# Gate and up weights of a mixture of experts in rows of 8 KB and units of 1 MB, with doubled slots and a router in natural column order

## The chip, the cores and the metric

The kernel runs on one core of a Trainium2 chip; the chip's other cores are idle. A core has TensorE (PE; its weight loads are listed as PEld), VectorE (DVE), ScalarE (ACT), GpSimd (POOL) and SyncE (SP), and 16 DMA engines that move data between HBM and the on-chip memory SBUF. The metric is the device time of one execution in microseconds (us), as the median of several runs.

## What is computed

The reference is one layer of a decoder trunk in float32, on 256 tokens of width 2048: adaLN vectors from `c`, four kinds of attention (A to D) that share one input and one output projection, and a mixture of 16 experts of width 512, of which each token uses 2. Cut to what matters here:

```python
sh1, sc1, g1, sh2, sc2, g2 = jnp.split(c_act @ ada_w[l] + ada_b[l], 6, axis=-1)
...
h = rmsnorm(x, norm2_g[l]) * (1.0 + sc2[:, None]) + sh2[:, None]
x = x + g2[:, None] * moe_ffn(h, router_w, router_bias, exp_w_gate[l], exp_w_up[l], exp_w_down[l])
...
aff = jax.nn.sigmoid((t @ router_w).astype(jnp.float32))
...
for e in range(N_EXPERTS):
    he = jax.nn.silu(t @ w_gate[e]) * (t @ w_up[e])
    y = y + combine[:, e:e + 1] * (he @ w_down[e])
```

The weights are read once: each expert has a gate, an up and a down matrix of 4.194 MB each, 201 MB for the 16; the other weights are some 165 MB.

## The kernel before

**The stream of weights.** All large weights come over SP's DMA queue in units of 512 KB (a tile of 128 partitions x 1024 float32, `UNIT`). The list `units` (lines 268 to 315) has their order: adaLN weights `ada_w` with the early projection pieces, then projections (`uw`), compression weights and the other adaLN vectors (`usc`, `ush`, `ug`) mixed, then the output projection (`uo`) with the last adaLN vector, and at the end, pair of experts by pair, `pair_units`: gate and up (`ugu`), then down (`udh`). The class `Stream` (line 101) hands out slots: `pump` takes the next unit of the list and a free slot and issues the load; `done` gives the slot back once the unit's last reader has been written into the program, and the load into a slot waits on the chip until those readers have run. The framework lays out the order on each engine's queue from a timeline that it works out itself, so SP's order follows the list only roughly. SP executes its queue in order, and eight loads can be under way.

**Slots.** `ring1` has 11 slots of one unit (`RING`, line 352). When an attention branch's score bias `T` isn't needed any more, its space becomes one slot of two units, three times (line 987). After attention come three slots `s0` to `s2` (line 1130), then five that are used once, in `yhl`, `yo`, `ga` and `gb` (`ONCE`, line 1223), whose space gets its proper use during the first pair, and after the output projection `y0` to `y2` (line 1261). A slot of two units is given back when both halves are done.

**Gate and up.** Line 181 views a gate matrix as 8 blocks c of 256 rows; partition p holds rows 2p and 2p + 1 of the block, one run of 4 KB in HBM. So k = 2c + i is the product over rows 256c + 2p + i. `GUORDER` (line 57) is the order of blocks c and matrices g (0 gate, 1 up). For each block and each of the pair's two experts there is one unit; the two experts' products run in the two halves of PE's columns (line 1423).

**Permuted columns.** Since k stands for every second row, all that meets these weights has the same order of the 2048 columns: the scale and shift `A2`, `B2` of the second norm (adaLN vectors `sc2`, `sh2`, made by `ada_cols` with a permuted bias `abP`), the router weights (`wrP`, permuted by four products with the identity in `permuted`, lines 407 and 1137), and the transposes of the router, which read every second column of `xt` (lines 1176 and 1199). After the router, `xsplit` (line 1333) scales x and splits it into two parts `xh` and `xl`; `xview` reads every second column. `gather` (line 1372) collects, for four experts at once, the tokens of each by a product with a 0/1 matrix, in steps of two k, and applies `A2` and `B2`; in the first pair these steps are mixed into the gate and up products.

**The end of a pair.** Silu and product, transposes `hpT`, the down products `dn` in four blocks of 512 columns, and `scatter` (line 1453), which adds the result to `xt`. The last pair's last block goes in pieces of 128 columns. `fgr`, the last gain, is spread over the partitions during the last pair, into two free slots.

Of the kernel before, what the change touches and what calls it, by code (L numbers as in the profile page):

```python
# [23 lines left out]
NE = 16  # L24
# [22 lines left out]
ONCE = ("yhl", "yhl", "yo", "ga", "gb")  # L47
# [9 lines left out]
GUORDER = [(c, g) for c in range(6) for g in range(2)] + [(6, 0), (7, 0), (6, 1), (7, 1)]  # L57
# [43 lines left out]
class Stream:  # L101
# [5 lines left out]
    def add_slots(self, pool, names, n=1):  # L107

        self.free += [(pool, t, n) for t in names]
        self.pump()  # L110

    def room(self, name):
        if isinstance(self.free[0], list):
            t, slot = self.free.pop(0)
            return t, slot
        pool, tag, n = self.free.pop(0)
        t = pool.tile([128, max(n, 1) * UNIT], F32, name=name, tag=tag, bufs=2 if tag == "yhl" else 1)
        slot = [pool, tag, n, n]
        self.free[0:0] = [[t[:, UNIT * i:UNIT * i + UNIT], slot] for i in range(1, n)]
        return t[:, 0:UNIT], slot  # L120

    def pump(self):
        while self.free and self.pos < len(self.units):
            key, load = self.units[self.pos]
            self.pos += 1
            if key is None:
                load()
                continue
            t, slot = self.room("u" + "".join(c for c in str(key) if c.isalnum()))
            load(t)  # L130
            self.live[key] = (t, slot)
# [18 lines left out]
def hybrid_trunk_kernel(  # L150
# [30 lines left out]
    gateT = exp_w_gate[0].rearrange("e (c p i) f -> p c e (i f)", p=128, i=2)  # L181
    upT = exp_w_up[0].rearrange("e (c p i) f -> p c e (i f)", p=128, i=2)
# [40 lines left out]
    def pair_units(p):  # L223
# [14 lines left out]
        us = [((("gu", p), c, g, e), mkg(c, g, e)) for c, g in GUORDER for e in range(2)]  # L238
# [113 lines left out]
    stream.add_slots(ring1, [f"r{i}" for i in range(RING)])  # L352
# [50 lines left out]


    abP = const.tile([128, 3, 16], F32, name="abP")

    def permuted(dst, src, m, tag):
        pp = ps(tag, [128, 2, 8, m], name="perm")
        for h in range(2):
            for i in range(2):  # L410
# [987 lines left out]
    for p in range(NP):  # L1398
# [3 lines left out]
        for n, (c, g) in enumerate(GUORDER):  # L1402
            if p == 0 and c < 6 and g == 0 or p == 0 and c == 6:
                next(first, None)
            if (c, g) == (6, 0):
                weights(p)
# [236 lines left out]
```

## Time and profile before

| | us |
|---|---|
| median of 3 runs (1059.71 to 1063.89) | 1061.38 |
| the profiled execution | 1063.05 |
| its span | 1061.3 |
| PE busy in the span | 965.6 (91%) |
| DVE, ACT busy | 516.6, 330.6 |
| read from HBM | 367.91 MB, 349 GB/s over the span |
| chain that ended last, by engine | PE 57%, DMA 28%, DVE 8%, ACT 3% |

The profile is of one execution. Times in it are us from the start of its span. The line of GB/s has 40 equal slices of 26.5 us. "The chain" is the work that ended last, followed back step by step to what released it. A wait is put down to what ended it. SPq is SP's queue of DMA issues. "x8" is a count. A tile is named without its numbers: `ugu` are all gate and up units.

### The profile page before, as it was taken

What the parts mean: (1) busy time and instruction counts of PE and PEld (TensorE: products, weight loads), DVE (VectorE), ACT (ScalarE), POOL (GpSimd) and SP (SyncE); (2) the same over time, 40 slices, a digit from 0 to 9 for tenths busy, and PEclk for the clock granted to TensorE, in tenths of its full rate; (3) what the DMA queues carried; (4) which work ended last, traced back from release to release, by engine and by line L of the source; (5) the groups of instructions that cost most, each with busy time, mean ns of one, the idle gap of its engine ahead of it and who ended that gap; (6) DMA issues with size and microseconds to landing.
All of it is one profiled execution on the core that took longest, in us unless ns stands there. A gap on an engine that the chain in (4) does not pass through costs nothing.

```text
span 1061.3 us, 16623 instructions
## 1 busy us (share of the span) xinstructions
PE 965.6 (91%) x6433; PEld 587.5 (55%) x6433; DVE 516.6 (49%) x1093; ACT 330.6 (31%) x710; POOL 4.8 (0%) x14
## 2 busy tenths in 40 slices
PE   5999989899889999979998999999989896998884
PEld 1677778898778986646794434433343332432222
DVE  2444557996899999544345232414133130413115
ACT  3333334455565757634334100100020000200013
POOL 0000000000000000000000000000000000000000
PEclk9999999899989999989998999999999999999997
DMA  9999999996999999999743999999999999999994
GB/s 330 356 358 358 353 318 304 332 360 217 318 352 327 334 348 385 349 304 382 274 150 114 410 408 409 409 409 409 409 409 409 409 408 409 409 410 409 409 387 135
DMA packets 172031, 371.18 MB, mean 350 GB/s; under 512 B 13561, under 2 KB 92322, under 8 KB 171690
## 3 DMA queue, kind: packets, MB, share of 16 engines
q1 hardware_dynamic: 170944, 368.42, 94.6%
q10 hardware_dynamic: 938, 1.61, 0.4%
q8 instruction: 53, 0.87, 0.3%
q14 instruction: 32, 0.26, 0.1%
q0 software_dynamic: 64, 0.02, 0.0%
HBM read 367.91 MB, written 2.10 MB: 349 GB/s over the span
## 4 chain that ended last, share of the span: by engine, by line
PE 57%; DMA 28%; DVE 8%; ACT 3%; issue 3%; SPq 0%; DVEq 0%; ACTq 0%
DMA ugu<-in_exp_w_up_dram 10%; DMA ugu<-in_exp_w_gate_dram 7%; PE dn L170 7%; PE acc L537 5%; PE acc L538 4%; PE acc L539 4%; DMA udh<-in_exp_w_down_dram 4%; PE ada L170 3%; PE gatep L170 3%; PE upp L170 3%; PE oacc L541 3%; PE oacc L542 3%; PE oacc L543 3%; DMA uw<-in_w_in_dram 2%; PE pg L1381 2%
## 5 line engine op out<-in xcount | busy, mean ns | idle before, releaser
L537 PE MATMUL acc<-Hh,wlo 128*128 128x256 f32 x512 | 148.2, 300 | 6.6 <-DVE wlo L562 4.2
L538 PE MATMUL acc<-Hl,whi 128*128 128x256 f32 x512 | 147.4, 290 | 0.0
L539 PE MATMUL acc<-Hh,whi 128*128 128x256 f32 x512 | 146.6, 289 | 0.0
L173 PE MATMUL gatep<-ugu,xg 128*64 128x512 f32 x364 | 122.6, 600 | 0.0
L173 PE MATMUL upp<-ugu,xg 128*64 128x512 f32 x368 | 121.2, 595 | 0.0
L170 PE MATMUL dn<-udh,heT 128*64 128x512 f32 x242 | 112.1, 600 | 2.9 <-DVE heT L1451 2.6
L537 PEld LDWEIGHTS acc<-Hh,wlo 128*128 128x128 f32 x512 | 98.7, 198 | 18.9 <-DVE wlo L562 6.7
L173 PE MATMUL dn<-udh,heT 128*64 128x512 f32 x234 | 108.3, 600 | 0.0
L538 PEld LDWEIGHTS acc<-Hl,whi 128*128 128x128 f32 x512 | 100.2, 196 | 3.4 <-issue 2.9
L539 PEld LDWEIGHTS acc<-Hh,whi 128*128 128x128 f32 x512 | 99.7, 195 | 2.5 <-issue 2.2
L1434 DVE TENSOR_TENSOR he<-upp,sg 128x128 f32<-128x128 f32 x32 | 7.1, 284 | 170.6 <-PE upp L173 167.9
L562 DVE TENSOR_TENSOR wlo<-uw,whi 128x1024 fp32r<-128x1024 f32 x62 | 75.7, 1221 | 15.8 <-ACT whi L560 15.6
L170 PE MATMUL gatep<-ugu,xg 128*64 128x512 f32 x144 | 75.2, 611 | 7.6 <-DMA ugu<-in_exp_w_gate_dram 7.6
L170 PE MATMUL upp<-ugu,xg 128*64 128x512 f32 x144 | 73.6, 600 | 7.8 <-DMA ugu<-in_exp_w_up_dram 7.8
L560 ACT CAST whi<-uw 128x1024 fp32r<-128x1024 f32 x62 | 64.8, 1047 | 48.7 <-PE acc L539 21.4
L1464 DVE TENSOR_TENSOR xt<-xt,sco 128x512 f32<-128x512 f32 (+1 forms) x70 | 42.3, 639 | 54.7 <-PE sco L1463 54.2
L1513 ACT CAST yhl<-yo 128x512 fp32r<-128x512 f32 x31 | 19.2, 618 | 159.7 <-DVE yo L1507 153.3
L170 PEld LDWEIGHTS dn<-udh,heT 128*64 128x64 f32 x242 | 30.0, 136 | 62.1 <-issue 49.1
L562 DVE TENSOR_TENSOR wlo<-uo,whi 128x1024 fp32r<-128x1024 f32 x31 | 37.8, 1223 | 51.2 <-ACT whi L560 49.4
L541 PE MATMUL oacc<-wlo,Oh 128*128 128x512 f32 (+1 forms) x160 | 57.8, 362 | 0.0
L542 PE MATMUL oacc<-whi,Ol 128*128 128x512 f32 (+1 forms) x160 | 56.0, 350 | 0.0
L543 PE MATMUL oacc<-whi,Oh 128*128 128x512 f32 (+1 forms) x160 | 55.9, 350 | 0.0
(397 smaller groups left out, 1730.0 us busy)
## 6 DMA issues: line engine op xcount, KB each, us to landing
ugu<-in_exp_w_up_dram SPq DMA_DIRECT2D x128, 512.0 KB, 10.2
ugu<-in_exp_w_gate_dram SPq DMA_DIRECT2D x127, 512.0 KB, 10.2
udh<-in_exp_w_down_dram SPq DMA_DIRECT2D x119, 512.0 KB, 10.2
usc<-in_ada_w_dram SPq DMA_DIRECT2D x64, 512.0 KB, 7.8
ush<-in_ada_w_dram SPq DMA_DIRECT2D x62, 512.0 KB, 7.1
uw<-in_w_in_dram SPq DMA_DIRECT2D x62, 512.0 KB, 6.0
ug<-in_ada_w_dram SPq DMA_DIRECT2D x56, 512.0 KB, 7.2
uo<-in_w_out_dram SPq DMA_DIRECT2D x31, 512.0 KB, 9.6
```

The costliest lines, as they stand in the source:

```text
L170: ins = op(*args, **kw).ins
L173: ins = op(*args, **kw).ins
L537: ins = mm(o, wl, hh, start=first, stop=False)
L538: mm(o, wh, hl, start=False, stop=False)
L539: mm(o, wh, hh, start=False, stop=last)
L541: ins = mm(o, hh, wl, start=first, stop=False)
L542: mm(o, hl, wh, start=False, stop=False)
L543: mm(o, hh, wh, start=False, stop=last)
L560: A.copy(hi, w)
L562: V.tensor_tensor(lo, w, hi[:].bitcast(F32), OP.subtract)
L1381: mm(pg[:, i, :], x_[:, t, i, 128 * c:128 * c + 128], oh4[q][:, t].rearrange("p e s -> p (e s)"), start=n == 0, stop=n == 3)
L1464: V.tensor_tensor(y(t, cs), y(t, cs), o, OP.add)
```

## The change

It does five things.

- Gate and up matrices are viewed as 4 blocks of 512 rows, with four rows to a partition: one run of 8 KB in HBM. A unit is 1 MB and fills a slot of two units; down units stay at 512 KB. `GUORDER` becomes (0, gate), (0, up), (1, gate), (1, up), (2, gate), (3, gate), (2, up), (3, up).
- `Stream` knows sizes. `ring1` has 5 slots of two units and one of one unit; `s0`, `y0` and `y1` are slots of two units, and so are `yhl` and `g2r`, which are used once. The total of 23 units in slots that come back stays; those used once are 4 units, not 5. A unit of 512 KB takes half a slot of two units, or the single slot.
- Where nothing fits a gate or up unit, `pump` stops until something does.
- The router works in natural column order. The permutation of the router weights and of three vectors at the start is gone; instead `A2` and `B2` are permuted after the adaLN vectors are known, each by 16 products with 32 columns of the identity. The router's transposes read 128 adjacent columns.
- `xview` reads every fourth column, `xh` and `xl` are laid out in four quarters, and a step of `gather` still makes two k; in the first pair the steps now stand before k = 0, 2 and so on of the gate blocks.

Its core:

```diff
-ONCE = ("yhl", "yhl", "yo", "ga", "gb")
+ONCE = ("yhl", "g2r")
...
-GUORDER = [(c, g) for c in range(6) for g in range(2)] + [(6, 0), (7, 0), (6, 1), (7, 1)]
+GUORDER = [(c, g) for c in range(2) for g in range(2)] + [(2, 0), (3, 0), (2, 1), (3, 1)]
...
+    def room(self, name, size=1):
+
+        for at, slot in enumerate(self.free):
+            if isinstance(slot, list) if size == 1 else not isinstance(slot, list) and slot[2] == size:
+                break
+            if size == 1 and not isinstance(slot, list):
+                break
+        else:
+            return None
+        if isinstance(slot, list):
+            return self.free.pop(at)
+        pool, tag, n, once = self.free.pop(at)
+        t = pool.tile([128, n * UNIT], F32, name=name, tag=tag, bufs=1)
+        slot = [pool, tag, n, once, n // size]
+        if size == n:
+            return [t[:], slot]
+        self.free[at:at] = [[t[:, UNIT * i:UNIT * i + UNIT], slot] for i in range(1, n)]
+        return [t[:, 0:UNIT], slot]
...
-        slot[3] -= 1
-        if not slot[3] and slot[2]:
-            self.free.append(tuple(slot[:3]))
+        slot[4] -= 1
+        if not slot[4] and not slot[3]:
+            self.free.append(tuple(slot[:4]))
             self.pump()
...
-    gateT = exp_w_gate[0].rearrange("e (c p i) f -> p c e (i f)", p=128, i=2)
-    upT = exp_w_up[0].rearrange("e (c p i) f -> p c e (i f)", p=128, i=2)
+    gateT = exp_w_gate[0].rearrange("e (c p i) f -> p c e (i f)", p=128, i=4)
+    upT = exp_w_up[0].rearrange("e (c p i) f -> p c e (i f)", p=128, i=4)
...
-        us = [((("gu", p), c, g, e), mkg(c, g, e)) for c, g in GUORDER for e in range(2)]
+        us = [((("gu", p), c, g, e), mkg(c, g, e), 2) for c, g in GUORDER for e in range(2)]
...
-    stream.add_slots(ring1, [f"r{i}" for i in range(RING)])
+    stream.add_slots(ring1, [f"r{i}" for i in range(RING // 2)], 2)
+    stream.add_slots(ring1, [f"r{i}" for i in range(RING // 2, RING // 2 + RING % 2)])
...
-    permuted(abP[:, 0, :].unsqueeze(2), abT[:, 48:64].unsqueeze(2), 1, "PT")
-    permuted(abP[:, 1, :].unsqueeze(2), abT[:, 64:80].unsqueeze(2), 1, "PT")
-    permuted(abP[:, 2, :].unsqueeze(2), g2n.unsqueeze(2), 1, "PT")
+    def permuted(dst, src, tag):
+
+        pp = ps(tag, [128, 4, 4], name="perm")
+        for i in range(4):
+            for h in range(4):
+                mm(pp[32 * h:32 * h + 32, i], ident[:, i:128:4], src[:, h:16:4], start=True, stop=True,
+                   tile_position=(0, 32 * h))
+        V.tensor_copy(dst.rearrange("p (c i) -> p i c", i=4), pp[:])
...
-        stream.add_slots(late, [f"s{i}" for i in range(LATE)])
+        work = late.tile([128, 8, 256], F32, name="work", tag="y0")
+        tms, x1q = work[:, 0:4].rearrange("p (t a) n -> p t (a n)", t=2), work[:, 4:8]
+        stream.add_slots(late, ["s0"], 2)
...
-        permuted(wrP[:], wr, NE, "pv")
+        permuted(A2[:], A2n[:], "pv")
+        permuted(B2[:], B2n[:], "pv")
...
-                                xt[:, t, 256 * (k // 2) + i:256 * (k // 2) + 256:2], ident)
+                                xt[:, t, 128 * k:128 * k + 128], ident)
...
-    stream.add_slots(late, ["y0", "y1", "y2"])
+    stream.add_slots(late, ["y0", "y1"], 2)
...
     def xview(t, c):
-        return xt[:, t, 256 * c:256 * c + 256].rearrange("p (m i) -> p i m", i=2)
+        return xt[:, t, 512 * (c // 2):512 * (c // 2) + 512].rearrange("p (m i) -> p i m", i=4)[:, 2 * (c % 2):2 * (c % 2) + 2]
...
-            for i in range(2):
-                k = 2 * c + i
-                if not p:
+            for i in range(4):
+                k = 4 * c + i
+                if not p and not g and not i % 2:
+                    next(first, None)
+                if not p or i == 2:
                     bt = Batch()
                 for e in (1, 0):
                     w = stream.get(keys[e])[:, 512 * i:512 * i + 512]
```

## Rows read from the trace of the kernel before

**Rows 1.** The page's second part: the span in 40 equal slices; what the DMA engines moved in each, in GB/s.

```profile
GB/s 330 356 358 358 353 318 304 332 360 217 318 352 327 334 348 385 349 304 382 274 150 114 410 408 409 409 409 409 409 409 409 409 408 409 409 410 409 409 387 135
```

**Rows 2.** The view of windows. A row has the stretch in us, its length, busy us and instructions (x) of PE, PEld, DVE, ACT and POOL, the granted clock of PE as a share, the DMA engines' share, and GB/s. The last two rows are from a second answer, of two short stretches.

```profile
500.00:565.00 65.00, 60.86 (x381) 50.16 (x380) 31.05 (x65) 30.34 (x55) 0.00 (x0) 0.95 0.62 216
565.00:580.00 15.00, 15.00 (x71) 7.42 (x72) 6.64 (x18) 3.94 (x8) 0.00 (x0) 0.86 0.22 71
...
600.00:1000.00 400.00, 369.99 (x1690) 141.99 (x1684) 105.54 (x205) 36.58 (x61) 0.00 (x0) 0.99 1.03 409
...
607.00:613.00 6.00, 5.09 (x26) 2.14 (x27) 1.64 (x6) 0.46 (x1) 0.00 (x0) 1.00 1.03 411
667.00:674.00 7.00, 6.42 (x38) 3.60 (x39) 1.84 (x4) 1.13 (x2) 0.00 (x0) 1.00 1.03 410
```

**Rows 3.** The DMA view of the stretch from 600 to 1000 us: packets and bytes with sizes, the queue of SP with the time of its packets as a share of 16 engines' time, and one issue row (KB each, median us from issue to landing).

```profile
DMA packets 44856, 163.54 MB, mean 409 GB/s; under 512 B 4983, under 2 KB 4983, under 8 KB 44834
...
q1 hardware_dynamic: 44834, 163.25, 102.4%
...
ugu<-in_exp_w_gate_dram SPq DMA_DIRECT2D x108, 512.0 KB, 10.2
```

**Rows 4.** The chain that ended last, in order of time, for the whole span: start in us, us taken, what. Seven pieces between 270 and 480 us are DMAs: 271.45, 277.87, 287.22, 311.22, 374.16, 408.55 and 468.31; four of them are shown.

```profile
271.45 4.26 DMA uw<-in_w_in_dram
...
277.87 4.63 DMA uw<-in_w_in_dram
...
311.22 4.27 DMA uw<-in_w_in_dram
...
468.31 5.99 DMA ug<-in_ada_w_dram
...
492.46 0.95 PE PT L1175 x8
...
731.60 10.16 DMA ugu<-in_exp_w_up_dram
```

**Rows 5.** The waits of SP's queue between 600 and 1000 us, longest in total first: who waited for what, us in total, times, longest. The rows that name a DMA are 6, with 242 us in all.

```profile
SPq L225 <- DMA ugu<-in_exp_w_gate_dram: 62.1, 72, 1.1
...
SPq L225 <- PE dn L173: 25.3, 22, 4.8
```

**Rows 6.** The DMA view of the stretch from 12 to 15 us, in which x is loaded: the same columns as in rows 3.

```profile
DMA packets 173, 1.26 MB, mean 419 GB/s; under 512 B 17, under 2 KB 20, under 8 KB 20
...
q1 hardware_dynamic: 173, 1.26, 101.0%
```

**Rows 7.** The timeline of SP's queue, in three stretches: start, us from the first issue to the end of the last, engine, line, operation, what is loaded, count.

```profile
242.38 17.61 SPq L188 DMA_DIRECT2D ush<-in_ada_w_dram  x5
...
574.85 2.06 SPq L225 DMA_DIRECT2D ugu<-in_exp_w_up_dram  x2
579.80 0.33 SPq L228 DMA_DIRECT2D udh<-in_exp_w_down_dram  x1
580.22 0.86 SPq L225 DMA_DIRECT2D ugu<-in_exp_w_up_dram  x2
...
606.80 0.42 SPq L225 DMA_DIRECT2D ugu<-in_exp_w_up_dram  x1
612.09 0.33 SPq L225 DMA_DIRECT2D ugu<-in_exp_w_gate_dram  x1
...
667.57 6.14 SPq L225 DMA_DIRECT2D ugu<-in_exp_w_gate_dram  x2
```

**Rows 8.** The chain from 560 to 605 us, in order of time, columns as in rows 4. One k of one matrix, for both experts, is two rounds of 0.43 us (a float32 product is two instructions); so 4 k of one matrix are 8 rounds.

```profile
559.77 3.72 ACT xh L1338 x9
...
567.41 1.05 PE gatep L170
...
569.68 0.43 PE upp L170
...
571.82 1.14 PE pg L1381 x8
```

**Rows 9.** The instructions of line 225, which issues the gate and up units: count, ns (least, median, most), first and last start; and the time from issue to landing.

```profile
L225 SPq DMA_DIRECT2D ugu<-in_exp_w_up_dram x128: 327/328/1037, 475.1 to 1008.2; - x128
...
DMA to landing us min/median/max: 3.2/10.2/11.4
```

**Rows 10.** The timeline of ACT and of PE, two rows that end a wait for a DMA: idle us before the row in brackets, and what ended it. From 264 to 295 us ACT has five such rows, with 1.1 to 2.9 us each.

```profile
268.72 1.05 ACT L560 CAST whi<-uw 128x1024 fp32r<-128x1024 f32 x1 [1.30 <-DMA uw<-in_w_in_dram]
...
474.35 1.06 PE L170 MATMUL ada<-ug,cB 128*32 128x512 f32 x1 [4.18 <-DMA ug<-in_ada_w_dram]
```

**Rows 11.** Instructions of single lines, columns as in rows 9: the permutations (three vectors at the start, the router weights later), ACT's split of x, and a plain cast of ACT of the same size.

```profile
L411 PE MATMUL perm<-rT,ident x16: 254/254/276, 5.0 to 5.8; 128*64 128x8 f32 x16
...
L411 PE MATMUL perm<-pkc,ident x8: 272/273/327, 467.3 to 467.7; 128*64 128x128 f32 x8
...
L1338 ACT ACTIVATE xh<-xt,rs x14: 503/511/522, 559.7 to 565.1; 128x256 fp32r<-128x256 f32 x14
...
L603 ACT CAST Hh<-hs x16: 400/406/410, 30.1 to 149.9; 128x256 fp32r<-128x256 f32 x16
```

**Rows 12.** The chain at the end of the span, columns as in rows 4.

```profile
1012.05 0.64 PE gatep L170
...
1022.62 0.89 PE upp L173 x5
```

More of the change, by code (lines that the diff above doesn't have):

```diff
@@ L105, in __init__, with add_slots @@
         self.units, self.pos, self.free, self.live = units, 0, [], {}
-    def add_slots(self, pool, names, n=1):
-        self.free += [(pool, t, n) for t in names]
+    def add_slots(self, pool, names, n=1, once=False):
+        self.free += [(pool, t, n, once) for t in names]
         self.pump()
[L112 to L120, printed above, removed]
+    def room(self, name, size=1):
[15 more added lines that the diff above has]
+        return [t[:, 0:UNIT], slot]
     def pump(self):
         while self.free and self.pos < len(self.units):
-            key, load = self.units[self.pos]
-            self.pos += 1
+            key, load = self.units[self.pos][0:2]
             if key is None:
+                self.pos += 1
                 load()
                 continue
-            t, slot = self.room("u" + "".join(c for c in str(key) if c.isalnum()))
-            load(t)
-            self.live[key] = (t, slot)
+            got = self.room("u" + "".join(c for c in str(key) if c.isalnum()), *self.units[self.pos][2:])
+            if got is None:
+                return
+            self.pos += 1
+            load(got[0])
+            self.live[key] = got
     def spare(self, name):
@@ L1168, in router_part @@
     def router_part(n):
-        x1T = late.tile([128, 4, 256], F32, name="x1T", tag="y2")
+        x1T = x1q
         for kk in range(0, 4, 2):
@@ L1194, in logits @@
                     behind(ins, opened)
-        x1T = late.tile([128, 4, 256], F32, name="x1T", tag="y2")
+        x1T = x1q
         px = ps("PT", [128, 2, 256])
@@ L1222, in hybrid_trunk_kernel @@
             once.append(1)
-            stream.add_slots(late, ONCE, 0)
+            stream.add_slots(late, ONCE, 2, True)
         for ii in range(i, min(i + SPLITS, len(opieces))):
@@ L1396, in hybrid_trunk_kernel @@
     ssy = const.tile([128, 2, 7], F32, name="ssy")
-    fgr, g2r = [], []
+    fgr = []
     for p in range(NP):
@@ L1402, in hybrid_trunk_kernel @@
         for n, (c, g) in enumerate(GUORDER):
-            if p == 0 and c < 6 and g == 0 or p == 0 and c == 6:
-                next(first, None)
-            if (c, g) == (6, 0):
+            if n == 5:
                 weights(p)
-            if p == 0 and n in (6, 8, 10, 12):
-                b = n // 2 - 3
-                if b % 2 == 0:
-                    g2r.append(late.tile([128, 1024], F32, name="g2r", tag=ONCE[3 + b // 2]))
-                spread(g2c[:, 4 * b:4 * b + 4], g2r[-1][:, 512 * (b % 2):512 * (b % 2) + 512])
+            if p == 0 and n > 3:
+                b = n - 4
+                if b == 0:
+                    g2r = late.tile([128, D], F32, name="g2r", tag="g2r")
+                spread(g2c[:, 4 * b:4 * b + 4], g2r[:, 512 * b:512 * b + 512])
             o = (gp, up)[g]
```

65 lines of the change are left out of this document (27 added, 38 removed).

## The prediction

> **What bounds the kernel now.** I read the slices first. The line of GB/s shows three states: 300 to 385 while adaLN, projections and attention run, a hole in the three slices from about 500 us, and one even rate from there almost to the end [rows 1]. The windows put numbers on it, and show PE busy nearly everywhere, so that its busy share alone decides nothing [rows 2]: 216 GB/s from 500 to 565 us, 71 GB/s from 565 to 580, then 409 GB/s over the 400 us from 600 to 1000 with the engines' share at 1.03. From 600 on the weight stream is the limit: PE is busy 370 of those 400 us, its idle time ends in waits for weights, and the chain there runs from DMA to DMA [rows 3, 4]. A loaded unit lands 10.2 us after its issue and eight are under way, one landing every 1.28 us; SP waits almost only for the eighth last transfer to land, seldom for a slot [rows 3, 5]. Each transfer's fixed cost is hidden, and only the rate of the packets counts.
>
> Before 500 us DMA is near its rate too, but the chain is mostly PE, ACT and DVE, with a DMA on it now and then [rows 4].
>
> **Step 1, the rows.** Gate and up go from 4 KB to 8 KB per packet; down stays at 4 KB. The trace holds 8 KB packets in one place, the two loads of x at the start. From 12 to 15 us, 153 of 173 packets are of 8 KB, and the rate is 419 GB/s; from 600 to 1000 us, with 4 KB packets, it is 409 [rows 3, 6]. Both are full queues. The gate and up bytes that stream while DMA is the limit are those of pairs 1 to 7 (pair 0's are in, or under way, when the experts begin): 7 pairs x 2 experts x 2 matrices x 4.194 MB = 117.4 MB. At 409 GB/s they take 287.1 us, at 419 they take 280.3: **-6.9 us**. Bounds: at no gain in rate, 0. By packet time instead of rate, a 4 KB packet takes 102.4% x 16 x 400 us / 39,851 = 164.5 ns, two 329 ns, an 8 KB one 101.0% x 16 x 3 us / 153 = 317 ns; that is 3.7% less, or -10.6 us. I take the rate, since bytes over time is what the stage waits for, while packet times overlap (their share is over 100%).
>
> The Trainium skill ("DMA: Bandwidth & Descriptors", Why small descriptors are slow) gives each packet a fixed overhead of about 3 bus cycles, with 32 bytes a cycle. By that a 4 KB packet costs 131 cycles and two of them 262 against 259, an estimate of 1.1%, and the sum would hold -3.3 us in place of -6.9. The rows of x show more than twice that, and I go by the rows.
>
> PE can take the faster stream: 370 us of work fits in the 393 us that would be left of those 400 [rows 2]. SP issues half as many gate and up transfers; each takes it 0.33 us out of 1.28 [rows 9], which was hidden and gains nothing.
>
> **Step 2, the restart of the stream.** Before, the first expert units fill every slot and SP stands still until PE gives one back: 5 units sit in slots used once, 23 in slots that come back, 28 in all. The first matmul of the experts is at 567.4 us; SP issues two units at 574.85, more at 579.80 and 580.22, and from there the queue is never empty [rows 7, 8]. After, a gate or up unit fits only a double slot: 5 doubles of ring1, 3 of T, s0, y0, y1 and two used once are 13 MB, or 26 old units; the single slot stays out. So 2 units fewer are in, worth 2.6 us at 1.28. But the slots used once now hold the gate of c = 0 alone, so the first slots to come back are those of its up units, after 4 k of gate and up: 16 rounds of 0.43 us and one gather of 1.14 us after 567.4 is 575.4, and then 2 MB come back at once, where before 1 MB had by 577 [rows 7, 8]. The gate of c = 1 follows after 2 gathers and 8 rounds, near 581. Issued by 577 us are 30 old units against 30 before, by 581.5 34 against 33. I put the balance at **0**, bounds -1 to +2.6.
>
> Later the slots could run out: at 606.80 and 667.57 SP stops until 612.09 and 673.4, since all are full, while the queue still holds work: the windows over both stops show 410 GB/s [rows 2, 7]. Some 10.2 us of queue stood when SP stopped, the stops last 5 to 6 us, and a unit alone needs at least 3.2 us to land [rows 9], so 1 to 2 us of cover are left. One slot fewer for gate and up (the single) costs 1.28 us of that, and a double comes back up to 0.9 us later: it holds, just. If it doesn't, two stops of 1 to 2 us are added: 0, up to +4.
>
> **Step 3, pairs of slots in the first 500 us.** Here ring1 changes from 11 single slots to 5 doubles and a single. 512 KB units go into halves, and a double comes back only when both tenants are done. The first half's successor waits for the other half: one unit more, 0.524 MB at some 357 GB/s or 1.5 us [rows 1], and from 242 to 260 us, where SP gets five slots in 17.6 us, about 4.4 [rows 7]. SP issues in order, so projection pieces queued behind are late too, and ACT's casts wait for those (268.72 us), PE's adaLN matmuls for others (474.35) [rows 10]. A delay counts only where a DMA is on the chain and has no queue ahead. The seven DMAs of this stretch on the chain take 4.3 us and more from issue to landing [rows 4]; a lone unit takes 3.2 or more [rows 9], so the three of 4.3 to 4.6 us have no cover and the others some. Half of them are first halves: 3 x 0.5 x 1.5 = 2.2, say **+2 us**. Upper bound 7 x 1.5 = +10.5. A lower bound below nothing can't be excluded, as every engine's order is laid out anew with the change; I put it at -2.
>
> **Step 4, the router.** Gone: 3 permutations at the start (24 PE instructions while PE waits for the first weights) and that of the router weights (8 instructions, 0.67 us, at 467 us, before a PE wait of 4.2 us for adaLN weights) [rows 10, 11]. Added there: 2 x 16 tiny matmuls, 64 instructions; at the 0.05 us a start of the same permutation at the beginning that is 3.2 us, which fits into that wait. Without the cover it is +3.2. The added copies are two of 16 columns, DVE being idle there. The 32 transposes no longer read every second column: eight of them take 0.95 us on the chain [rows 4], so even half of that gone from all would be -1.9; nothing says that the step costs anything, and I take 0. The split of x now reads every fourth column, not every second, and it stands on the chain just before the experts [rows 8]. ACT's split takes 511 ns at a step of two, a plain cast 406 [rows 11]; if a step of four costs the same 105 ns once more, nine of them are +0.9; if not, 0. I take 0 for the whole of step 4: bounds -1.9 to +4.1.
>
> **Step 5, the end.** PE runs without a gap from 1012.05, when a gate unit lands, to the last output; the gate and up units behind it are in by 1018.4 (the last issue, 1008.2, and 10.2) [rows 9, 12]. So the end follows the landing of the last pair's gate and up weights, and the gain of step 1 arrives whole. With 1 MB units PE starts the last up block when 2 MB are in instead of 1 MB, 1.7 us more work behind the last landing, but PE ends gate and up at 1023.5, 5 us behind it, with the products for fgr in between, and these can go ahead of the last block: 0, bounds -1 to +1.7.
>
> **Sum.** -6.9 + 0 + 2 + 0 + 0 = -4.9 us. The profiled execution took 1063.05 us with a span of 1061.3; it would take 1058.15. It lies 1.67 us over the median of 1061.38, so I predict **1056.5 us**. A measurement of this kernel can tell about 0.5%, 5.3 us, from no change: faster is under 1056.1, slower over 1066.7.
>
> **The rivals.**
> - A, the whole gain: rows of 8 KB give 2.4 to 3.7% and the pairs cost nothing, -6.9 to -10.6: 1050.8 to 1054.5. For it: packet times, and a first stretch whose queue is mostly deep. Against it: the bare DMAs on the chain. Chance 0.24.
> - B, the change doesn't do what it says: 8 KB packets go no faster than 4 KB ones in a long stream, and x's 3 us are the mild start of a queue. Then 0, or half of it, -3.4, and +2: 1060 to 1063.4. For it: 4 KB packets come near the same rate already; against it: 10 GB/s between two full queues. Chance 0.20. The rule of the Trainium skill named in step 1 would end here too.
> - C, slower: the pairs starve SP in the first 500 us. Place: 240 to 300 us and 440 to 475 us, where SP already waits for slots. Price: five of the seven DMAs on the chain pushed by 1.5 us, two by 4.4, and the cover of the router's 64 instructions gone: 5 x 1.5 + 2 x 4.4 + 3.2 = 19.5, less 6.9: 1074. It decides for slower once the first 565 us grow by 12. For it: the slice of 217 GB/s from 239 us; against it: the slices of over 350 around it, in which the queue stays full [rows 1]. Chance 0.11.
> - My own case, 1053 to 1060, has 0.45; about half of it lies under 1056.1.
>
> **How the numbers follow.** Faster: 0.24 from A and about 0.21 from my case, 0.45. Slower: C, and a little of B with step 2 gone wrong, 0.12. Same: 0.43. The range takes in most of A and B and leaves C out: 1050 to 1065.
>
> **What would show it.** Step 1: packets of 8 KB in the expert stage and, while gate and up stream, some 419 GB/s; over a mix with a third of down, 415 to 416. If the rate stays at 409, B is right. Step 2: the first issue after the hole near 575 us, a rate that stays full at the pair ends. Step 3: the first expert matmul near 569 rather than 567 us; a later one than 579 is C. Step 4: no PE gap that grows around 467 to 475 us. The prediction is wrong where the start of the experts moves by more than 5 us either way, or where DMA idles after 600 us.

## The result, and the profile after

The changed kernel takes **1076.32 us** (median of 4 runs, 1073.03 to 1077.0); the kernel before, beside it, 1061.48. The ratio is 1.0128, 95% interval 1.0104 to 1.0151: slower by 1.3%, where 0.5% faster was predicted (1056.5, range 1050 to 1065). The profiled execution has a span of 1074.2 us, 12.9 more than before. The slices answer to [rows 1]:

```profile
GB/s 328 358 359 357 332 298 237 328 350 178 375 331 373 335 300 357 387 239 383 274 164 117 339 408 418 410 420 414 421 409 422 414 418 417 415 419 413 421 348 133
```

Two things differ. In the first 500 us there are deeper dips, and the even rate that began in the 23rd slice before is reached only in the 24th; from there it is higher, at 408 to 422 in place of 408 to 410. The DMA view from 600 to 1000 us shows the cause of the higher rate (columns as in [rows 3]):

```profile
DMA packets 30848, 165.77 MB, mean 414 GB/s; under 512 B 3425, under 2 KB 3425, under 8 KB 17830
...
q1 hardware_dynamic: 30829, 165.50, 101.5%
...
ugu<-in_exp_w_gate_dram SPq DMA_DIRECT2D x54, 1024.0 KB, 13.8
```

Of 30,848 packets 13,018 are now of 8 KB; before there were 22 that long [rows 3]. Where the time went is on the chain (columns as in [rows 4, 8, 12]):

```profile
475.22 5.25 DMA uo<-in_ada_w_dram
...
580.30 1.05 PE gatep L182
...
1010.51 16.50 DMA ugu<-in_exp_w_up_dram
1027.06 1.50 PE upp L185 x5
```

The first matmul of the experts is at 580.30 us; before it was at 567.41 [rows 8]. That is 12.9 us, the whole loss. From there to the end it is 494 us in both kernels (1074.2 - 580.3 and 1061.3 - 567.4). So there are two questions: what delays the start of the experts, and why a faster stream saves nothing behind it. Windows of the changed kernel, relative to its first expert matmul, 40, 40 and 320 us long, and then to the end (columns as in [rows 2]):

```profile
580.20:620.20 40.00, 40.00 (x195) 16.79 (x196) 12.78 (x28) 8.96 (x15) 0.00 (x0) 0.98 0.66 250
620.20:660.20 40.00, 39.48 (x186) 15.57 (x184) 13.59 (x27) 3.06 (x5) 0.00 (x0) 1.00 1.02 420
660.20:980.20 320.00, 288.34 (x1336) 111.00 (x1334) 79.07 (x157) 29.16 (x50) 0.00 (x0) 1.00 1.02 416
980.20:1074.20 94.00, 75.73 (x362) 28.37 (x356) 30.82 (x67) 14.69 (x35) 0.00 (x0) 0.94 0.83 317
```

The same four of the kernel before:

```profile
567.30:607.30 40.00, 40.00 (x207) 18.25 (x206) 9.71 (x27) 7.84 (x14) 0.00 (x0) 0.98 0.75 285
607.30:647.30 40.00, 39.09 (x180) 14.91 (x179) 13.78 (x27) 2.63 (x5) 0.00 (x0) 1.00 1.03 409
647.30:967.30 320.00, 293.71 (x1350) 114.73 (x1349) 80.64 (x160) 29.17 (x50) 0.00 (x0) 0.99 1.03 409
967.30:1061.30 94.00, 71.22 (x342) 25.04 (x338) 30.43 (x64) 14.80 (x35) 0.00 (x0) 0.94 0.86 325
```

Rate times length gives megabytes: in the first 40 us the changed kernel moves 10.0 in place of 11.4, then 16.8 in place of 16.4, then 133.1 in place of 130.9. It loses 1.4 MB at the restart and wins 2.6 MB in the next 360 us by its rate.

### The profile page after: what moved, and what is told of

The parts are those of the page before. It is cut to its first block, busy times and chain, and to the rows that moved or that the text cites. A ratio compares the mean times of both kernels' runs of the same rounds, so it can differ in the third digit from the quotient of the medians.

```text
span 1074.2 us, 16322 instructions
## 1 busy us (share of the span) xinstructions
PE 970.1 (90%) x6465; PEld 589.8 (55%) x6465; DVE 516.8 (48%) x1091; ACT 334.6 (31%) x710; POOL 4.8 (0%) x14
## 4 chain that ended last, share of the span: by engine, by line
PE 68%; DMA 16%; DVE 8%; ACT 4%; issue 2%; SPq 0%; DVEq 0%; ACTq 0%
PE dn L182 10%; DMA ugu<-in_exp_w_up_dram 10%; PE acc L542 5%; PE acc L543 5%; PE acc L544 5%; PE gatep L182 4%; PE upp L182 4%; PE upp L185 4%; PE ada L182 3%; PE pg L1388 3%; PE oacc L546 3%; PE oacc L548 3%; PE oacc L547 3%; DMA uw<-in_w_in_dram 3%; PE gatep L185 2%
## 5 line engine op out<-in xcount | busy, mean ns | idle before, releaser
L542 PE MATMUL acc<-Hh,wlo 128*128 128x256 f32 x512 | 149.2, 300 | 16.4 <-DVE wlo L567 13.5
L185 PE MATMUL upp<-ugu,xg 128*64 128x512 f32 x368 | 117.4, 596 | 6.7 <-DMA ugu<-in_exp_w_up_dram 6.7
L185 PE MATMUL gatep<-ugu,xg 128*64 128x512 f32 x368 | 118.0, 598 | 1.4 <-DMA ugu<-in_exp_w_gate_dram 1.4
L182 PE MATMUL upp<-ugu,xg 128*64 128x512 f32 x144 | 73.8, 598 | 6.2 <-DMA ugu<-in_exp_w_up_dram 6.2
L182 PE MATMUL gatep<-ugu,xg 128*64 128x512 f32 x144 | 74.7, 606 | 2.8 <-DMA ugu<-in_exp_w_gate_dram 2.7
L185 PEld LDWEIGHTS upp<-ugu,xg 128*64 128x64 f32 x368 | 33.8, 137 | 46.4 <-issue 35.3
L1438 ACT ACTIVATE sg<-gatep 128x512 f32<-128x512 f32 x8 | 4.8, 597 | 162.9 <-PE gatep L185 162.9
L185 PEld LDWEIGHTS gatep<-ugu,xg 128*64 128x64 f32 x368 | 33.7, 137 | 36.9 <-issue 32.8
## 6 DMA issues: line engine op xcount, KB each, us to landing
ugu<-in_exp_w_gate_dram SPq DMA_DIRECT2D x64, 1024.0 KB, 13.6
udh<-in_exp_w_down_dram SPq DMA_DIRECT2D x120, 512.0 KB, 11.4
```

What stands on the lines that cost most here:

```text
L182: ins = op(*args, **kw).ins
L185: ins = op(*args, **kw).ins
L542: ins = mm(o, wl, hh, start=first, stop=False)
```

## The experiments

The theories. T1: slots of ring1 in pairs delay the start of the experts. Its rivals: the router's edits, or a layout of the engines' order that happened to come out worse. T2: rows of 8 KB do save what was forecast, and units of 1 MB take it back at the two ends of the stream. Its rival: the rate is worth nothing in time. "Start" is the first expert matmul, "stage" the time from it to the end of the span, both of the profiled execution; ratios are against the kernel before. The last two columns are the mean granted clock of PE in that execution, from 0 to the start and over the last 60 us.

| run | median us | ratio, 95% interval | start | stage | clock to start | clock at the end |
|---|---|---|---|---|---|---|
| before | 1061.48 | | 567.3 | 493.9 | 0.97 | 0.91 |
| after | 1076.32 | 1.0128, 1.0104 to 1.0151 | 580.2 | 494.0 | 0.94 | 0.91 |
| e1 before, ring in pairs | 1074.46 | 1.01, 1.007 to 1.0129 | 579.3 | 493.7 | 0.95 | 0.91 |
| e2 after, halves back singly | 1064.68 | 1.0022, 1.0 to 1.0044 | 571.3 | 496.2 | 0.97 | 0.86 |
| e3 after, 4 KB rows | 1080.03 | 1.0167, 1.0129 to 1.0204 | 575.7 | 501.6 | 0.97 | 0.91 |
| e4 before, router's edits | 1062.58 | 1.0002, 0.9982 to 1.0023 | 565.1 | 493.1 | 0.98 | 0.91 |
| e5 e2 and pair 0 in 512 KB | 1064.58 | 1.0023, 1.0004 to 1.0042 | 568.7 | 494.7 | 0.97 | 0.90 |
| e6 e5 and a third late slot | 1090.12 | 1.026, 1.0234 to 1.0286 | 569.7 | 515.3 | 0.97 | 0.89 |
| e7 before, two pairs | 1063.63 | 1.0014, 0.9994 to 1.0034 | 569.6 | 498.8 | 0.96 | 0.84 |
| e8 e5 and pairs 1, 7 in 512 KB | 1064.39 | 1.0024, 1.0006 to 1.0042 | 567.0 | 493.5 | 0.97 | 0.91 |
| e9 after, pair 7 in 512 KB | 1079.42 | 1.0145, 1.0114 to 1.0175 | 583.0 | 494.5 | 0.93 | 0.88 |
| e10 after, half of gate and up | 1036.96 | 0.9785, 0.9756 to 0.9813 | 579.2 | 456.6 | 0.96 | 0.92 |
| e11 after, pairs 6, 7 in 512 KB | 1073.23 | 1.0119, 1.0088 to 1.0149 | 576.9 | 492.2 | 0.97 | 0.92 |

**e1, the pairs alone.**

```diff
-    stream.add_slots(ring1, [f"r{i}" for i in range(RING)])
+    stream.add_slots(ring1, [f"r{i}" for i in range(RING // 2)], 2)
+    stream.add_slots(ring1, [f"r{i}" for i in range(RING // 2, RING // 2 + RING % 2)])
```

> The kernel before with one edit: of the 11 ring slots of the first stage, 10 are handed out as halves of five double slots and come free only when both halves have been consumed. Rows of 4 KB, router and order of the units as before. Theory (the pairs cost what was lost ahead of the experts): first expert matmul 8 to 13 us later than 567.4 (575 to 580), and the median near 1071 to 1075. Rival (the router's edits, or the order in which everything was laid out anew, cost it): first expert matmul within 3 us of 567.4, median 1060 to 1064.

The start is at 579.3 us and the ratio 1.01: one edit gives nearly the whole loss. The windows show where; first the kernel before, then e1, then the changed kernel:

```profile
140.00:240.00 100.00, 93.84 (x865) 84.12 (x865) 84.23 (x162) 45.87 (x99) 1.05 (x2) 0.95 0.99 336
360.00:440.00 80.00, 76.86 (x575) 60.45 (x578) 71.09 (x160) 51.08 (x125) 0.00 (x0) 1.00 1.01 360
```

```profile
140.00:240.00 100.00, 95.31 (x876) 84.09 (x876) 75.98 (x148) 43.42 (x88) 1.05 (x2) 0.94 0.88 296
360.00:440.00 80.00, 73.14 (x544) 61.24 (x543) 71.90 (x142) 48.00 (x110) 0.00 (x0) 0.98 0.94 334
```

```profile
140.00:240.00 100.00, 95.61 (x881) 84.62 (x880) 79.05 (x150) 44.45 (x91) 1.05 (x2) 0.95 0.90 306
360.00:440.00 80.00, 72.95 (x543) 59.58 (x545) 70.92 (x147) 47.09 (x108) 0.00 (x0) 0.98 0.94 333
```

Where DMA was full (0.99 and 1.01), it falls to 0.88 and 0.94. The loss is in the supply, and the other engines hardly show it: among PE's waits in the changed kernel from 60 to 600 us one row names a DMA, with 3.8 us, and from 60 to 565 us the rows of PE, DVE and ACT that name a DMA have 28.8 us in e1 and 27.6 before. So which late transfer holds up which engine stays open; that the pairing does it, e1 and e2 show. SP's waits between 140 and 240 us name the consumers that hold a slot (columns as in [rows 5]); e1, then the kernel before:

```profile
SPq L188 <- PE part L792: 8.1, 2, 7.4
SPq L206 <- DVE wlo L563: 7.9, 2, 5.9
SPq L206 <- DVE TB L533: 6.2, 1, 6.2
```

```profile
SPq L188 <- DVE ada_v L484: 16.8, 10, 6.3
...
SPq L206 <- DVE pc L847: 3.7, 1, 3.7
```

In e1 four rows have a single wait of 5.9 to 7.6 us; the kernel before has one such, of 6.3, and the next is 3.7.

**e2, halves handed back singly.** In the first stage a half goes back to the list as soon as its own unit is done; two free halves are joined again for a unit of the experts.

```diff
...
+        if slot[2] == 2 and not slot[3] and self.pos < self.early:
+            self.free.append([t, slot, "half"])
+            self.pump()
+            return
...
```

> The changed kernel, but in the first stage each half of a double slot is handed out again as soon as its own unit is consumed; two free halves are joined to one slot only for the 1 MB units of the experts. All else as changed. Theory: the first expert matmul returns from 580.3 to 567 to 570, the median from 1076 to 1062 to 1066 (the experts' stage keeps its 494 us). Rival (router or order): stays at 578 to 581 and 1074 to 1078.

From 140 to 240 us the rate is 334 GB/s again, from 360 to 440 it is 347, and the start is at 571.3 us. That is 9 of the 12.9 us, with everything else of the change in place; 567 to 570 was expected. A first stage with halves handed back was run four times, in e2, e5, e6 and e8 (not quite the same: e5, e6 and e8 load pair 0 in smaller units, e6 has one slot more): starts of 571.3, 568.7, 569.7 and 567.0, mean 569.2. That of the changed kernel ran five times, with e3, e9, e10 and e11: 580.2, 575.7, 583.0, 579.2 and 576.9, mean 579.0. So as run the pairs cost about **10 us**; single starts scatter by 3 to 4.

**The clock in these starts.** Much of that scatter goes with PE's granted clock. Windows from 0 to 40 us and from 0 to the first expert matmul (columns as in [rows 2]); the kernel before, the changed kernel, and e3, which changes nothing that runs before the first gate or up unit:

```profile
0.00:40.00 40.00, 27.62 (x237) 14.23 (x238) 12.90 (x46) 14.74 (x32) 1.73 (x8) 1.00 1.00 340
0.00:567.34 567.34, 521.61 (x4364) 414.61 (x4364) 382.06 (x816) 276.21 (x608) 4.80 (x14) 0.97 0.94 321
```

```profile
0.00:40.00 40.00, 25.52 (x203) 12.49 (x204) 11.31 (x41) 14.74 (x32) 1.73 (x8) 0.66 1.01 338
0.00:580.23 580.23, 526.55 (x4395) 418.11 (x4396) 380.62 (x813) 278.77 (x606) 4.78 (x14) 0.94 0.90 313
```

```profile
0.00:40.00 40.00, 26.48 (x218) 13.48 (x219) 13.03 (x45) 14.75 (x32) 1.73 (x8) 1.00 1.00 340
0.00:575.67 575.67, 521.36 (x4396) 414.32 (x4396) 379.81 (x813) 279.01 (x606) 4.78 (x14) 0.97 0.91 315
```

The five starts of the changed kernel's first stage stand in the order of their clock: 575.7 and 576.9 at 0.97 (e3, e11), 579.2 at 0.96 (e10), 580.2 at 0.94, 583.0 at 0.93 (e9). PE's idle time ahead of the start (length less busy) moves little within a group: 52.7 to 54.3 us in these five and e1, 44.7 to 50.4 in the other seven, with means of 53.6 and 47.8. So the pairs add some 6 us of idle time, and at a clock of 0.97 they cost **7.5 us** of start: 576.3 in the mean against 568.8 (before, e2, e5, e6, e8). Of the 12.9 us of the profiled executions, 4.9 are longer PE work, 526.6 us in place of 521.6, at the lower clock. e3 had a clock of 1.00 over the first 40 us where the changed kernel had 0.66, so that part needn't come from the change; whether the pairs lower the clock at all, these runs don't tell.

**e4, the router alone.** All router edits of the change in the kernel before (permutations of the two products in blocks of two).

```diff
...
-        permuted(wrP[:], wr, NE, "pv")
+        permuted(A2[:], A2n[:], "pv")
+        permuted(B2[:], B2n[:], "pv")
...
-                                xt[:, t, 256 * (k // 2) + i:256 * (k // 2) + 256:2], ident)
+                                xt[:, t, 128 * k:128 * k + 128], ident)
...
```

> The kernel before with the router's edits alone: products with A2 and B2 in natural column order, two small permutations of A2 and B2 after the attention in place of those of the bias, gain and router weights, transposes of contiguous 128 columns. Slots and rows as before. Theory: within 3 us of the kernel before (1060 to 1064), first expert matmul 565 to 570. Rival (the router's edits or the new layout of the work cost the 13 us): first expert matmul 575 to 581, median 1070 to 1076.

Ratio 1.0002, start 565.1 us. The rival falls, and that a mere new layout costs 13 us isn't borne out by this one. e4 reads every second column when it splits x, not every fourth as the change does; that part of the change is in e2, which starts 9 us earlier than the changed kernel all the same.

**e7, two pairs.** As e1, with `range(2)` doubles and seven singles.

> The kernel before with 2 of its 11 ring slots' doubles in place of 5: four of the slots are handed out as halves of two doubles, seven stay single. Theory (every pair costs the time that its first half lies idle, so the cost goes with their number): two fifths of the 12 us of five pairs, first expert matmul 570 to 574, median 1064 to 1068. Rival (a threshold: only when most of the ring is paired does the stream run dry): first expert matmul within 1.5 us of 567.4, median 1060 to 1062.

The start is 2.3 us later, just under what T1 asked for and inside the scatter; the median doesn't differ from before. Neither a cost in proportion to the pairs nor a threshold is shown. Its stage of 498.8 us is a warning: but for two paired slots the program from the start on is that of the kernel before, which took 493.9 (e1, with five pairs, 493.7). PE's clock over the last 60 us was 0.84 in place of 0.91. e2 (0.86) likewise has 496.2 us where the changed kernel has 494.0. So stages compare best at a like clock at the end, and differences of 2 us between single profiles prove little.

**e3, rows of 4 KB in slots of 1 MB.**

```diff
-            return lambda t: nc.sync.dma_start(t, (gateT, upT)[g][:, c, 2 * p + e])
+            def load(t):
+                for h in range(2):
+                    nc.sync.dma_start(t[:, UNIT * h:UNIT * h + UNIT], (gateT, upT)[g][:, c, 2 * p + e, UNIT * h:UNIT * h + UNIT])
+            return load
```

> The changed kernel, but each 1 MB unit of gate and up is loaded by two transfers of 512 KB with rows of 4 KB into the same slot. Theory (the 8 KB rows do give about 7 us over the seven pairs, which a slower restart takes back): the stretch 700 to 1000 us goes from 417 to 409 GB/s, the stage from the first expert matmul to the end from 494 to 499 to 502 us, the median to 1081 to 1084. Rival (the rate is worth nothing, since the matmuls bound the stage): the stage stays at 493 to 496 us and the median at 1075 to 1078.

The DMA view from 700 to 1000 us:

```profile
DMA packets 33599, 122.50 MB, mean 408 GB/s; under 512 B 3730, under 2 KB 3730, under 8 KB 33584
```

408 GB/s in place of 417, and a stage of 501.6 us in place of 494.0, at one clock (0.91 at the end). The rows of 8 KB are worth **7.5 us**. The median, 1080.03, lies under the 1081 to 1084 expected and only 3.7 us over the changed kernel's; the profiled execution started 4.5 us earlier. e3 halves the transfers along with the rows, so the runs don't part the two; the packet times under step 1 below speak for the rows. The price of the rest stands out here: with 4 KB rows in both, the stage is 7.7 us longer than in the kernel before. By e4 the router's edits aren't it, which leaves large slots (and the split of x, which no run takes alone).

**e5 and e8, where the price is paid.** e5 loads pair 0's gate and up in 512 KB units into halves; e8 does so for pairs 0, 1 and 7, and counts yo as one more slot. Both hand halves back throughout. From e8's edit (`SMALL = (0, 1, 7)`; in e5 the condition is `if p:`):

```diff
...
+        if p not in SMALL:
+            us = [((("gu", p), c, g, e), mkg(c, g, e), 2) for c, g in GUORDER for e in range(2)]
+        else:
+            us = [((("gu", p), c, g, e), mk0(c, g, e)) for c, g in GUORDER0 for e in range(2)]
...
```

> As the run before with the halves handed back singly (e2), and besides the gate and up weights of the first pair come in units of 512 KB again (rows of 4 KB, block by block of 256 rows, in half slots); pairs 1 to 7 keep rows of 8 KB and units of 1 MB. Theory (the 8 KB rows save about 7 us in pairs 1 to 7, and the first pair in units of 1 MB takes as much back: two half slots less are filled ahead, and the first slot comes back after 16 matmuls of 0.592 us in place of 12): the first slot comes back 7 to 8 us after the first expert matmul (9.5 in the changed kernel), the experts' stage takes 486 to 490 us in place of 494 to 496, median 1054 to 1060. Rival (the rate in the later pairs is worth nothing in time): stage 493 to 497, median 1061 to 1067.

The restart did improve (the first slot came back 7.5 us after the first expert matmul, as expected), and the stage did not: 494.7 us, a miss. The two windows that answer to the first two above:

```profile
568.70:608.70 40.00, 40.00 (x205) 17.95 (x205) 12.71 (x28) 9.10 (x16) 0.00 (x0) 0.98 0.79 303
608.70:648.70 40.00, 39.08 (x179) 15.18 (x179) 13.87 (x27) 2.93 (x5) 0.00 (x0) 1.00 0.89 361
```

12.1 MB in place of 10.0 come in the first 40 us, but 14.4 in place of 16.8 in the next: the stop has moved behind the first pair, to where the stream goes over from halves to whole slots. The largest row of SP's waits between 600 and 660 us stands at the line that issues whole units, and what it waits for are down products, whose weights sit in the halves:

```profile
SPq L252 <- PE dn L200: 15.8, 6, 7.0
```

The rival named the right time (493 to 497), but not for its reason: by e3 the rate is worth something, and a stop takes it back.

> As the run with the first pair in 512 KB units (e5), and besides pairs 1 and 7 come in units of 512 KB too, and the place of yo serves as one more slot that is used once; 8 KB rows and 1 MB units stay for pairs 2 to 6 only. Theory (the rate is worth about 1 us for each pair, and large units cost at the two ends of the stream: fewer slots filled ahead, a stop of about 7 us behind the first pair while slots wait for both halves, and at the end 16 matmuls in place of 8 behind the last landing): first expert matmul 566 to 569, stage 487 to 491 us, last landing of gate or up to the end 42 to 44 us, median 1054 to 1059. Rival (the rate in the middle is worth nothing in time): stage 493 to 496, median 1060 to 1064.

Stage 493.5 where 487 to 491 was expected: the rival's number again. In e8 the stop has moved once more, to between pairs 1 and 2:

```profile
607.00:647.00 40.00, 39.09 (x181) 14.95 (x182) 13.77 (x27) 2.83 (x5) 0.00 (x0) 1.00 1.01 391
647.00:727.00 80.00, 72.50 (x340) 29.33 (x338) 18.75 (x39) 8.07 (x14) 0.00 (x0) 0.98 0.96 385
727.00:967.00 240.00, 222.18 (x986) 87.34 (x982) 59.88 (x117) 21.11 (x36) 0.00 (x0) 0.99 1.02 417
```

24 GB/s under 409 for 80 us is 1.9 MB, or 4.7 us, and 18 under it for the 40 us ahead another 0.7 MB; the 240 us at 417 give 8 x 240 = 1.9 MB back. A gain and a loss of nearly one size, which the windows keep apart and the median doesn't.

**e6, a third late slot.**

```diff
...
         stream.add_slots(late, ["s0"], 2)
+        stream.add_slots(late, ["s2"])
...
-    stream.add_slots(late, ["y0", "y1"], 2)
+    stream.add_slots(late, ["y0"], 2)
+    stream.add_slots(late, ["y1"])
...
```

> As the run with the first pair in 512 KB units (e5), and besides the late pool gives the stream three single slots' room at the end of the attention (one double and one single), as the kernel before had, where the changed kernel has two; the other end pays with one slot less after the last block of the output projection. Theory (what is left ahead of the experts, 2 to 4 us, is the missing late slot): 440 to 500 us from 304 back to about 335 GB/s, first expert matmul 565 to 569, median 2 to 4 us below that run. Rival (it is scatter from execution to execution): first expert matmul and median as in that run, within 1 us.

A miss: the start stays (569.7), and the stage grows to 515.3 us. From 800 to 900 us e6 moves 386 GB/s, and the row with most of SP's waiting from 700 to 1000 us is for a slot; in e5 it is for a landing (39.3 us), and the one for this slot has 32.3:

```profile
SPq L252 <- PE gatep L200: 43.1, 9, 8.3
```

e6 has ten whole slots and three single ones that gate and up can't use, e5 eleven and one. That this one slot makes the 20 us is argued from the waits, not tried by itself.

**e10, how much a faster stream could give.** The second expert's gate and up of pairs 1 to 7 aren't loaded, and its products read the first expert's weights: all matmuls stay, and the layer isn't computed.

```diff
...
-        us = [((("gu", p), c, g, e), mkg(c, g, e), 2) for c, g in GUORDER for e in range(2)]
+        us = [((("gu", p), c, g, e), mkg(c, g, e), 2) for c, g in GUORDER for e in range(1 if HALF[0] <= p <= HALF[1] else 2)]
...
-                    w = stream.get(keys[e])[:, 512 * i:512 * i + 512]
+                    w = stream.get(keys[e % len(keys)])[:, 512 * i:512 * i + 512]
...
```

> The changed kernel, but in pairs 1 to 7 the gate and up weights of the second expert of a pair aren't loaded: its matmuls read the first expert's slot. All matmuls stay, 58.7 of the 117.4 MB of gate and up of those pairs are left out. Theory (the matmuls and what they wait for on the other engines take nearly as long as the stream, so a faster stream can give at most the 17 us that TensorE waits for transfers): stage from first expert matmul to the end 474 to 482 us in place of 494, no waits for gate or up weights after the first pairs, first expert matmul as in the changed kernel. Rival (the stream alone bounds the stage, the matmuls have room): stage below 470 us.

The stage falls to 456.6 us, far under what I expected, and as the rival said: with the stream at 303 to 331 GB/s PE has 97 to 99 of every 100 us busy.

```profile
900.00:1000.00 100.00, 99.10 (x452) 36.93 (x453) 28.61 (x56) 10.04 (x17) 0.00 (x0) 1.00 0.83 303
```

So the matmuls leave 37 us of room, and the waits for weights that the profile shows (17 us in the changed kernel) are not a measure of it. The idea that PE is nearly a second bound falls; the stream is the limit, and the bytes decide.

**e9 and e11, the end.** e9 brings pair 7's gate and up in 512 KB units, e11 those of pairs 6 and 7 (`SMALL = (7,)` and `(6, 7)`).

> The changed kernel, but the gate and up weights of the last pair come in units of 512 KB with rows of 4 KB again, in halves of the same slots; all ahead of it as changed. Theory (1 MB units cost about 4 us at the end: 47 us from the last landing of gate or up to the end in place of 43): the stage from first expert matmul to the end falls from 494 to 489 to 492 us, last landing to the end 42 to 45 us, median 1071 to 1074. Rival (the end costs nothing, and the last pair loses 1 us of rate): stage 494 to 496, median 1076 to 1078.

> The changed kernel, but the gate and up weights of the last two pairs come in units of 512 KB with rows of 4 KB. Theory (with units of 1 MB TensorE finishes every pair about 4 to 5 us later behind the same stream, since 16 matmuls in place of 8 stand behind a landing; this lag of pair 6 runs through the last pair, where in the run with the last pair alone in 512 KB TensorE never waited): pair 6 ends its gate and up matmuls 391 to 394 us after the first expert matmul in place of 396.0, the last pair 452 to 455 in place of 456.3, stage 490 to 493 us. Rival (the lag comes from elsewhere): pair 6 at 395 to 398, stage 494 to 497 us.

e9 gains nothing: 494.5 us, the rival's number (its clock at the end, 0.88, may hide 1 to 2 us, an estimate from e2 and e7). On its chain PE works from 995 us almost to the end without waiting for weights; it is late with the work of pair 6.

```profile
994.88 1.66 PE dn L184 x4
...
1011.43 1.28 PE upp L187 x5
1013.14 1.28 PE gatep L187 x5
```

In e11 the chain at the end goes by DMAs of 10 us, as before:

```profile
1005.78 10.15 DMA ugu<-in_exp_w_gate_dram
1015.99 10.16 DMA ugu<-in_exp_w_up_dram
```

The last gate or up matmul of each pair, in us after the first expert matmul (start of the last one in the trace):

| | pair 5 | pair 6 | pair 7 | end |
|---|---|---|---|---|
| before | 330.8 | 391.4 | 455.6 | 493.9 |
| after | 334.5 | 396.0 | 456.3 | 494.0 |
| e9 | 334.4 | 395.9 | 456.7 | 494.5 |
| e11 | 334.1 | 394.0 | 453.5 | 492.2 |

e11 meets its theory in all three numbers. It gives up the rate of two pairs, 2 x 7.5 / 7 = 2.1 us, and still ends 1.8 earlier: 1 MB units at the end cost 3.9 us by this pair of profiles. The gain is no larger than what single profiles scatter: e2, whose stage is the changed kernel's, ends pair 6 at 394.8 us.

## Why the prediction was wrong

| step | predicted us (bounds) | measured us | by |
|---|---|---|---|
| 1 rows | -6.9 (-10.6 to 0) | -7.5 | e3 |
| 2 restart | 0 (-1 to +2.6, and up to +4 later) | +4.7 | worked out from windows |
| 3 pairs | +2 (-2 to +10.5) | +10 to +12, at one clock +6 to +8 | e1, e2, all starts |
| 4 router | 0 (-1.9 to +4.1) | 0, within 0.2% | e4 |
| 5 end | 0 (-1 to +1.7) | +3 to +4 | e3 less step 2, e11 |

**Step 3 is the one that failed**, in its size: +2 where it was +10 to +12 as run, and +6 to +8 at one clock. Its mechanism was right, a half waits for its neighbour; the count was wrong. It priced three of the seven DMAs that stood on the chain [rows 4] (all seven for its upper bound), 1.5 us each, and left the rest uncosted, because DMA's rate in this stretch is high [rows 1]. But that rate needed the slots: with eleven the engines were at 0.99, with five doubles and a single at 0.88. What is lost is bytes everywhere in the stretch, and they come out as a later start, not as longer pieces of the old chain. Case C had the sign, the total (1074) and the starting point (a start later than 579), at a chance of 0.11. The total was luck: it added 19.5 us of delays and took off 6.9 of rate, where the start came 12.9 later, part of that with the clock, and the rate was lost again behind it. Its places were 240 to 300 and 440 to 475 us, the dips of [rows 1]; most was lost from 140 to 240 and 360 to 440 us, where the slices showed a full queue and I had counted that against C.

**Step 2 failed too.** SP's timeline of the changed kernel (columns as in [rows 7]):

```profile
534.38 0.33 SPq L240 DMA_DIRECT2D udh<-in_exp_w_down_dram  x1
...
570.05 0.33 SPq L237 DMA_DIRECT2D ugu<-in_exp_w_gate_dram  x1
589.77 0.81 SPq L237 DMA_DIRECT2D ugu<-in_exp_w_up_dram  x2
598.04 0.80 SPq L240 DMA_DIRECT2D udh<-in_exp_w_down_dram  x2
```

The single slot did not stay empty, a down unit went into it: 27 old units were in, not 26. But the first slots came back 9.5 us after the first expert matmul (589.77 - 580.30), where the step had 8.0, and the next ones 17.7 us after it, where it had 13.6, the gate of c = 1 alone: PE takes gate and up of one c in turns, so both come back nearly together (598.04 and 599.75). The 8.0 took every round at 0.43 us, though [rows 8] shows the first at 1.05; in the changed kernel too the first takes 1.05 on the chain. One unit fewer (0.5 MB) and 1.4 MB less in the first 40 us are 1.9 MB, 4.7 us at 409 GB/s. No run takes this price away alone: in e5 and e8 smaller units for the first pairs only move the stop to where the stream goes over to whole slots. So the split of e3's 7.7 us into restart and end is worked out, not tried.

**Step 1 held**, and nearly to the microsecond: 416 to 417 GB/s over the mix against the 415 to 416 named, from a view of three microseconds in which 8 KB packets ran [rows 6]. From 408 to 417 over a mix with a third of down is 2.2%, so about 3.3% on gate and up, more than the 2.4% of the step. From 700 to 707.5 us the changed kernel's queue holds, but for the smallest, 8 KB packets alone:

```profile
DMA packets 435, 3.17 MB, mean 423 GB/s; under 512 B 48, under 2 KB 48, under 8 KB 48
```

By the step's own working, with 164.5 ns for a 4 KB packet, 101.5% x 16 x 400 us, less 14,405 such packets, leave 317 ns for each of the 13,018 of 8 KB, as in the load of x, against 329 for two short ones. That the sum came out near is luck in part: at 3.3% it would be 9.2 us, and why e3 shows 7.5 of them stays open. The rule of the Trainium skill ("DMA: Bandwidth & Descriptors", Why small descriptors are slow), an estimate of 1.1% by its 3 cycles for each packet, is too small here.

**Step 5** took the bare last landing and let the gain arrive whole. The lag is older than the last block: behind 1 MB units PE ends pair 6 at 394.8 to 396.0 us (after, e2, e9), behind 512 KB units at 391.0 to 393.3 (before, e1, e4, e7), and carries that into the last pair. Its upper bound of 1.7 was too small.

**Step 4** held within what can be told. The split of x at a step of four costs more than the 105 ns that the step feared, 737 ns in place of 511, but two such pieces stand on the changed kernel's chain ahead of the experts (`570.86 1.28 ACT xh L1347 x2`), not nine [rows 8].

So -7.5 of rate, +4.7 at the restart and about +3 at the end leave the stage at 494 us, and the later start remains: the pairs, and in the profiled executions some 4 to 5 us that went with the lower clock. Between the mean start of the versions with halves handed back (569.2) and those of before and e4 (567.3 and 565.1) 3 us are left; PE's idle time doesn't show them (47.7 us in the mean with halves handed back, 48.0 in before, e4 and e7), so they may be scatter, and e6 did not settle it. Of the versions that load every weight none is faster than the kernel before.

## What to carry to other kernels

When slots are joined to larger ones, ask everywhere the slots are used what it does to the number of transfers that can be under way, above all where the queue looks full: it may be full because of the slots. A larger unit saves by its rate for each byte, but it is paid once at each end of a stream (later return of the first slots, more matmuls behind a landing), so set the gain over the whole stream against some 8 us here. When a total doesn't move, take megabytes in windows that start at the same event in both traces: they part a gain and a loss that cancel. Before you explain a few microseconds between two single profiles, compare the granted clock of the stretch, and the engine's idle time beside its busy time.

## What the runs showed of the hardware

- Long transfers of 4 KB packets ran at 408 to 409 GB/s (e3, before), 8 KB packets alone at 423 (changed kernel, 700 to 707.5 us), with the 16 engines full in both (shares of 1.02 to 1.03 over the stage).
- A unit of 1 MB landed 13.8 (gate) or 14.9 us (up) after its issue, one of 512 KB 10.2 in the kernel before. At 414 and 409 GB/s that is 5.7 to 6.2 and 4.2 MB under way, an estimate, or 5 to 6 units and 8.
- Five executions of one first stage reached the first expert matmul between 575.7 and 583.0 us, in the order of PE's mean granted clock, 0.97 to 0.93. Over the first 40 us it was 1.00 in three of them, 0.70 and 0.66 in the others.
- TensorE, given weights enough, was granted 1.00 of its clock and worked 97 to 99 of 100 us (e10, 600 to 1000 us).
